# Spatial gating moved from the projection phase into the attention phase of a hybrid encoder step, with attention cut into sections of 1024 keys

## The chip, the cores and the metric

The kernel runs on one core of a Trainium2 chip. The metric is the device time of one launch in microseconds, the median of the runs shown. The program is one straight list of instructions on five queues: PE (TensorE), DVE (VectorE), ACT (ScalarE), POOL (GpSimd) and SP, which issues every DMA. Each queue runs in order. A build-time scheduler puts the instructions of each engine into that order, starting from the order in which the Python code emits them.

## What is computed

One layer on 2176 tokens: 128 sample tokens (8 streams of 16 steps, each with 512 cached keys) and a prompt of 2048 tokens. D_MODEL is 1024, the two head groups are 512 wide each, D_FF is 2816.

```python
h = rms_norm(x); p = h @ w_in                  # columns: u | v | q | k | v of attention, 512 each
u_a = gelu(p[u]); v_a = layer_norm(gelu(p[v]))
out_a = u_a * (tril(W_s) @ v_a + b_s)          # per head of 128, in chunks of 128 tokens
z = q @ k.T / 8                                # 8 heads of 64, strictly causal
log_fail = where(reach, log_sigmoid(-z), 0)
incl = cumsum(log_fail, axis=keys, reverse=True)   # excl: the same, one key later
w = where(reach, exp(log_sigmoid(z) + excl), 0); out_b = w @ v
mix = concat(rms_norm(out_a), rms_norm(out_b)) @ w_out
x = x + rms_norm(mix)
up = causal_conv3(rms_norm(x) @ w_up)
y = x + rms_norm((gelu(up[gate]) * up[val]) @ w_down)
```

The kernel forms the attention weights without logarithms: s = sigmoid(z), S = 1 - s, a running product of S from the last key backwards, and w = s times that product one key later.

## The kernel before

Activations are feature-major (features on the 128 partitions, tokens along the free axis), and the tokens go through in pieces of 384 (the last has 256). A float32 product of the projections is three passes: each operand is split into hi + lo, hi by a cast on ACT and lo by a subtraction on DVE (`weights`, lines 174 and 175, for weight tiles; lines 161 and 162 for the token-major stage).

Phase 1 (from line 287) is a list of jobs; the weights of a job are fetched and split two jobs ahead, and chains of small steps advance one step after each job. For each piece the jobs are: four u jobs (`feature`, evacuated by `evac_u`, lines 396 to 401), eight token-major jobs for the gating values v (`evac_va`, with their LayerNorm), eight for the attention values, then eight feature-major jobs for k and q (`evac_qk`), whose halves are stored to DRAM. `gate_chain` (lines 441 to 470) then does the spatial mixing of the piece on PE (psg, line 447), multiplies by u on DVE, norms the result over its 512 features and stores it, split, to the DRAM array na_s.

Phase 2 (from line 541) is attention. For each of four pairs of heads (hp), query tiles of 128 are taken in the order of `ORDER`, which alternates short and long ones; a unit is one query tile of one head, with up to 2048 keys. A unit has four stages, run as a pipeline over the units: loads four units ahead; `weigh` (line 550); transposes of the weights three units later (line 580); the values of two query tiles and both heads after that (line 715). In `weigh` PE writes scores of 512 keys to PSUM (line 688), ACT takes the sigmoid (line 560), POOL clears the masked triangle of the last 128 keys (`affine_select`, line 692) and writes S = 1 - s (line 563), DVE runs one running product over the whole row (the scan, line 567) and multiplies by s (line 568). The scan reads S twice from SBUF; the multiplication reads s and S; both of POOL's steps read and write SBUF.

Eight sample units, one per stream, stand among the units of the first three head pairs (three, three and two of them). Their values (line 649) multiply weight tiles of 128x128 by 64 columns, in 40 instructions on PE.

Phase 3 is the output projection, its norm and the residual; its first operands come from na_s and from ob_s, the stored attention output (`mix_prep_chain`, line 797). Phase 4 is the convolutional FFN. These two are not changed, but for the name of an array.

Of the kernel before, what the change touches and what calls it, by code (L numbers as in the profile page):

```python
# [21 lines left out]
P = 128  # L22
# [16 lines left out]
ORDER = [0, 8, 9, 1, 10, 2, 11, 3, 12, 4, 13, 5, 14, 6, 15, 7]  # L39
# [13 lines left out]
def hybrid_kernel(ctx: ExitStack, tc: tile.TileContext, a: dict):  # L53
# [27 lines left out]
    # sample queries and keys, split, kept for the sample attention  # L81
    qs = cpool.tile([P, 2, 4, NSAMP], F32R, name="qs")
    ks = cpool.tile([P, 2, 4, NSAMP], F32R, name="ks")

    class Scratch:
        """a DRAM array cut along its token axis, so that a reader waits for its own tokens only."""
# [8 lines left out]
        def parts(self, c0, c1):  # L95
            """(array of those tokens, first, last + 1, counted from c0)"""
# [12 lines left out]
    na_s = dpool.tile([2, 4, P, TOK], F32R, name="na_s")  # L109
# [5 lines left out]
    # Products run as a list of jobs; a job's weights are fetched and split two jobs ahead, and  # L115
    # the chains of small steps (norms, gating) advance by one step after each job.
# [11 lines left out]
    def store(out, in_, then=None, wait=1):  # L128
        """a store, issued some steps later, so that loads behind it don't wait for its data."""
# [27 lines left out]
    def split(pool, src, shape, tag, bufs=None):  # L157
        """src = hi + lo exactly, both in float32r."""
# [19 lines left out]
    def sq_sum(pool, key, acc, src, first, n):  # L178
        """acc[P, n] (+)= sum over the 4 feature tiles of src[P, 4, n] squared."""
# [59 lines left out]
    def sq_step(pool, key, acc, src, first, n, eng=None):  # L239
        """acc[P, n] (+)= src[P, n] squared."""  # L240
# [20 lines left out]
    # keys [hi; lo] of a head and queries, as [hi; hi] and as [lo; lo]; opened when room is there  # L261
# [11 lines left out]
    def key_tile(h):  # L273
        """three tiles take turns; the last heads leave one in kq free early."""
# [3 lines left out]
    def load_queries(h, c):  # L278
        t = kq[0].tile([P, 2, 512], F32R, tag="Q", name="Q", bufs=4)
        for src, o0, o1 in q_s[h // 2].parts(NSAMP + c * 512, NSAMP + (c + 1) * 512):  # L280
# [6 lines left out]
    # ------------------------------------------------------------------ phase 1  # L287
    # input projection, spatial gating; the RMSNorm's row factor is applied to the products
    with ExitStack() as c1:
# [54 lines left out]
        def piece_jobs(pi, H, Hn):  # L344
# [96 lines left out]
            def gate_chain():  # L441
# [18 lines left out]
                for f in range(4):  # L460
# [8 lines left out]
                    if f == 1:  # L469
                        yield  # L470
# [728 lines left out]
```

## Time and profile before

| | us |
|---|---|
| median of three runs (lowest, highest) | 3116.44 (3113.71, 3117.62) |
| span of the profiled execution, first to last instruction | 3110.4 |
| PE busy | 2894.4 (93%) |
| DVE busy | 1962.9 (63%) |
| ACT busy | 1203.9 (39%) |
| POOL busy | 806.8 (26%) |

The profiled execution is known by its span; the median of the runs is 6.0 us more than the span, which is what lies around it. The busy share is an average over phases with different limits: phase 1 ends with the last projection product at 529.6 us, phase 2 with the last attention values at 1259 us, phase 3 near 1500 us. A busy PE is not PE at its peak, since matmuls overlap in the pipeline. Idle time of an engine that is waited for by nobody costs nothing.

### The profile page before, as it was taken

How to read it: one execution, taken by the hardware profiler on the slowest of the kernel's cores; microseconds unless marked ns; L12 is line 12 of the kernel's file. 1: busy time of each engine (PE TensorE's matmuls, PEld its weight loads, DVE VectorE, ACT ScalarE, POOL GpSimd, SP SyncE). 2: the span in 40 equal slices, each digit the busy share in tenths (PEclk: the TensorE clock that was granted, in tenths of full speed). 3: DMA queues.
4: the chain of work that ended last, by engine and by line, in shares of the span. 5: the costliest groups of instructions: out<-in, count | busy, mean ns of one | idle time of the engine just before them, and what ended most of it. 6: DMA issues, size and time to landing. Idle time of an engine off the chain costs nothing.

```text
span 3110.4 us, 43545 instructions
## 1 busy us (share of the span) xinstructions
PE 2894.4 (93%) x17064; PEld 2718.8 (87%) x17064; DVE 1962.9 (63%) x2667; ACT 1203.9 (39%) x2068; POOL 806.8 (26%) x874
## 2 busy tenths in 40 slices
PE   8999997788797786999999999999999999999997
PEld 8999996666676654899999999999999999999997
DVE  6676776878878788586645455673544566344445
ACT  5444443444444354454433223433322243332222
POOL 1000002877858789256100000210000031000002
PEclk9999998788887798999999999999999999999998
DMA  5666677114142310566421221253122224212223
GB/s 203 219 211 223 234 248 213 48 61 109 50 116 62 99 48 21 182 208 222 152 80 53 70 75 62 88 160 100 57 69 72 65 87 130 73 55 68 72 64 105
DMA packets 192542, 352.88 MB, mean 113 GB/s; under 512 B 24785, under 2 KB 116177, under 8 KB 190289
## 3 DMA queue, kind: packets, MB, share of 16 engines
q1 hardware_dynamic: 192336, 350.09, 35.4%
q8 instruction: 135, 2.21, 0.3%
q14 instruction: 71, 0.57, 0.1%
HBM read 286.97 MB, written 63.06 MB: 113 GB/s over the span
## 4 chain that ended last, share of the span: by engine, by line
PE 75%; POOL 10%; DVE 6%; DMA 4%; issue 2%; ACT 1%; SPq 0%; POOLq 0%; ACTq 0%; DVEq 0%
PE pu L258 11%; PE pu L259 11%; PE pu L257 11%; POOL S L563 7%; PE pd L257 5%; PE pd L259 5%; PE pd L258 5%; PE psf L259 3%; PE psf L257 3%; PE psf L258 3%; PE po L649 2%; POOL s L692 2%; PE po L715 2%; PE pst L387 2%; PE pst L389 2%
## 5 line engine op out<-in xcount | busy, mean ns | idle before, releaser
L175 DVE TENSOR_TENSOR wlo<-wr,whi 128x1024 fp32r<-128x1024 f32 (+2 forms) x357 | 392.4, 1100 | 562.3 <-ACT whi L174 560.3
L257 PE MATMUL pu<-hhi,whi 128*128 128x364 f32 (+1 forms) x2112 | 695.6, 329 | 1.0 <-ACT nhs L983 1.0
L258 PE MATMUL pu<-hlo,whi 128*128 128x364 f32 (+1 forms) x2112 | 696.2, 330 | 0.0
L259 PE MATMUL pu<-hhi,wlo 128*128 128x364 f32 (+1 forms) x2112 | 695.8, 330 | 0.4 <-DVE wlo L175 0.4
L174 ACT CAST whi<-wr 128x1024 fp32r<-128x1024 f32 (+2 forms) x357 | 330.5, 926 | 739.0 <-PE pu L258 277.9
L563 POOL TENSOR_SCALAR S<-s 128x512 f32<-128x512 f32 (+4 forms) x336 | 400.3, 1202 | 123.5 <-ACT s L560 100.6
L567 DVE TENSOR_TENSOR_SCAN S<-S 128x256 f32<-128x256 f32 (+16 forms) x136 | 349.6, 2579 | 94.3 <-POOL S L563 67.5
L257 PEld LDWEIGHTS pu<-hhi,whi 128*128 128x128 f32 x2112 | 399.3, 189 | 1.6 <-ACT nhs L983 1.6
L258 PEld LDWEIGHTS pu<-hlo,whi 128*128 128x128 f32 x2112 | 398.6, 189 | 0.2 <-POOL hlo L783 0.2
L259 PEld LDWEIGHTS pu<-hhi,wlo 128*128 128x128 f32 x2112 | 398.0, 188 | 0.8 <-DVE wlo L175 0.7
L257 PE MATMUL pd<-ghi,whi 128*128 128x362 f32 (+3 forms) x1016 | 337.0, 332 | 10.7 <-DVE acc L1019 10.7
L259 PE MATMUL pd<-ghi,wlo 128*128 128x362 f32 (+3 forms) x1016 | 335.9, 331 | 0.0
L258 PE MATMUL pd<-glo,whi 128*128 128x362 f32 (+3 forms) x1016 | 335.8, 331 | 0.0
L586 ACT COPY wT<-pt 128x512 f32<-128x512 f32 (+3 forms) x328 | 165.5, 554 | 339.3 <-PE pt L580 336.0
L971 DVE SCALAR_TENSOR_TENSOR y<-pu,cvec,y 128x726 f32<-128x726 f32 (+2 forms) x352 | 270.0, 777 | 8.7 <-ACT y L968 4.1
L580 PE MATMUL pt<-ident,s 128*128 128x128 f32 (+1 forms) x1128 | 184.7, 308 | 92.3 <-DVE s L568 90.7
L580 PEld LDWEIGHTS pt<-ident,s 128*128 128x128 f32 (+1 forms) x1128 | 147.6, 158 | 123.4 <-issue 95.4
L783 POOL TENSOR_TENSOR hlo<-xp,hhi 128x182 fp32r<-128x182 f32 x32 | 22.2, 699 | 789.0 <-ACT hhi L782 407.9
L257 PEld LDWEIGHTS pd<-ghi,whi 128*128 128x128 f32 x1016 | 193.2, 190 | 14.1 <-DVE acc L1019 7.4
L1019 DVE TENSOR_TENSOR acc<-acc,pd 128x362 f32<-128x362 f32 (+2 forms) x192 | 101.7, 530 | 156.4 <-PE pd L259 155.7
L257 PE MATMUL psf<-hhi,whi 128*128 128x384 f32 (+1 forms) x576 | 191.0, 332 | 10.0 <-ACT hhi L314 7.2
L258 PEld LDWEIGHTS pd<-glo,whi 128*128 128x128 f32 x1016 | 193.2, 190 | 0.3
(173 smaller groups left out, 5083.1 us busy)
## 6 DMA issues: line engine op xcount, KB each, us to landing
wr<-wup SPq DMA_DIRECT2D x132, 512.0 KB, 3.3
wr<-win_f SPq DMA_DIRECT2D x72, 512.0 KB, 4.8
wk<-win_t SPq DMA_DIRECT2D x96, 256.0 KB, 2.8
wr<-wout SPq DMA_DIRECT2D x38, 512.0 KB, 4.1
wr<-wdown SPq DMA_DIRECT2D x72, 256.0 KB, 2.6
x<-xT SPq DMA_DIRECT2D x40, 384.0 KB, 5.6
wr<-wdown SPq DMA_DIRECT2D x48, 320.0 KB, 2.9
Q<-q_s SPq DMA_DIRECT2D x48, 256.0 KB, 8.2
```

Source lines behind the costliest of these rows:

```text
L174: nc.scalar.copy(hi, wr)
L175: nc.vector.tensor_tensor(out=lo, in0=wr, in1=hi.bitcast(F32), op=ALU.subtract)
L257: nc.tensor.matmul(ps, lhsT=whi, rhs=ahi, start=start, stop=False)
L258: nc.tensor.matmul(ps, lhsT=whi, rhs=alo, start=False, stop=False)
L259: nc.tensor.matmul(ps, lhsT=wlo, rhs=ahi, start=False, stop=stop)
L387: nc.tensor.matmul(pss[i], lhsT=hi, rhs=whi, start=(k == 0), stop=False)
L563: nc.gpsimd.tensor_scalar(out=S[:, c0:c0 + cn], in0=s[:, c0:c0 + cn], scalar1=-1.0, scalar2=1.0, op0=ALU.mult, op1=ALU.add)
L567: nc.vector.tensor_tensor_scan(out=R, data0=R, data1=R, initial=1.0, op0=ALU.mult, op1=ALU.bypass)
L580: nc.tensor.transpose(pt[:kn, j], w[:, (j0 + j) * P:(j0 + j) * P + kn], ident)
L586: nc.scalar.copy(wT[:, j0:j0 + full], pt[:, :full])
L971: nc.vector.scalar_tensor_tensor(out=o, in0=i, scalar=w, in1=o, op0=ALU.mult, op1=ALU.add)
L1019: nc.vector.tensor_tensor(out=o, in0=o, in1=src, op=ALU.add)
```

## The change

The u products leave phase 1, and with them `evac_u` and `gate_chain`. Phase 1 now begins each piece with the token-major jobs; the LayerNormed gating values go to a DRAM array va_s, and the row factors of all tokens are kept in the tile rall. In phase 2 a generator `gating` loads the u weights once, splits them with the norm gain folded in, and then takes the 17 token tiles of 128 one by one, token-major: load x, split it, 24 products of 512 columns, a scaling by the row factor, a gelu for three or four tiles at once; `gate_chain` then does mixing, the norm (its mean square by `bn_stats`, its square root on POOL) and a transposition on PE per tile. The generator is advanced between attention units, from the end of the first head pair on, in proportion to the keys that the units hold.

Attention takes the query tiles in pairs (`PAIRS`); a pair with more than 1024 keys is done in two sections of keys, the later keys first; the second section starts its running product from the value that the first left (a copy on DVE, a copy on POOL in place of a memset). All eight sample units stand in the first head pair, one after each pair of query tiles, and use the tiles of the gating generator, which begins after them. Their values go the other way round: weights of 32 columns as the stationary operand, 128 value columns moving, each of four groups into its own 32 partitions; a copy on ACT and one transposition on PE follow.

```diff
+PAIRS = [0, 4, 1, 5, 2, 6, 3, 7]
...
-            for f in range(4):
-                jobs.append(feature(f, lambda ps, f=f: when_ready(lambda: evac_u(f, ps))))
-            jobs += token(1, evac_va)
-            jobs += token(0, evac_v)
+            jobs += token(1, lambda i, ps: when_ready(lambda: evac_va(i, ps)))
+            jobs += token(0, lambda i, ps: when_ready(lambda: evac_v(i, ps)))
...
-        psz = c2.enter_context(tc.tile_pool(name="p2z", bufs=4, space=PSUM, reuse_waits="tile"))
-        pst = c2.enter_context(tc.tile_pool(name="p2t", bufs=3, space=PSUM, reuse_waits="tile"))
+        psz = c2.enter_context(tc.tile_pool(name="p2z", bufs=3, space=PSUM, reuse_waits="tile"))
+        pst = c2.enter_context(tc.tile_pool(name="p2t", bufs=2, space=PSUM, reuse_waits="tile"))
+        psf = c2.enter_context(tc.tile_pool(name="p2g", bufs=2, space=PSUM, reuse_waits="tile"))
...
-            big = W > 1024
-            s = two.tile([P, 2048 if big else 1024], F32, tag="sB" if big else "sS", name="s", bufs=3)
-            S = two.tile([P, 2056 if big else 1032], F32, tag="SB" if big else "SS", name="S")
+            s = two.tile([P, 1024], F32, tag="s", name="s", bufs=4)
+            S = two.tile([P, 1032], F32, tag="S", name="S", bufs=3)
...
-            nc.gpsimd.memset(S[:, W:W + 1], 1.0)
+            if carry is None:
+                nc.gpsimd.memset(S[:, W:W + 1], 1.0)
+            else:
+                nc.gpsimd.tensor_copy(S[:, W:W + 1], carry)
...
+            nc.vector.tensor_tensor_scan(out=R, data0=R, data1=R, initial=1.0 if carry is None else carry,
+                                         op0=ALU.mult, op1=ALU.bypass)
...
+                for j in range(5):
+                    kn = P if j < 4 else NS
+                    for kt in range(4):
+                        cs = slice(kt * P, (kt + 1) * P)
+                        nc.tensor.matmul(po[kt * 32:(kt + 1) * 32], lhsT=wT[:kn, j, kt * 32:(kt + 1) * 32],
+                                         rhs=vc[:, j, cs] if j < 4 else vnew[:, cs], start=(j == 0), stop=(j == 4))
...
+        def gate_chain(i, u):
+            vt = fil.tile([P, 512], F32, tag="va", name="va", bufs=2)
+            load(vt, va_s.parts(i * P, (i + 1) * P)[0][0])
+            yield
+            pm = psf.tile([P, 4, P], F32, tag="pf", name="pm")
+            for h in range(4):
+                nc.tensor.matmul(pm[:, h], lhsT=wst[:, kind, h], rhs=vt[:, h * P:(h + 1) * P], start=True, stop=True)
+            for h in range(4):
+                nc.vector.scalar_tensor_tensor(out=o[:, hs], in0=pm[:, h], scalar=bst[:, kind, h:h + 1],
+                                               in1=u[:, hs], op0=ALU.add, op1=ALU.mult)
+            nc.vector.bn_stats(out=six, in_=o)
+            nc.vector.bn_aggr(out=mv, in_=six)
...
+            nc.gpsimd.tensor_tensor(out=rs, in0=ms, in1=mhalf[:, 0:1], op=ALU.pow)
+            yield
+            nc.vector.scalar_tensor_tensor(out=o, in0=o, scalar=rs, in1=ga, op0=ALU.mult, op1=ALU.mult)
+            yield
+            for h in range(4):
+                nc.tensor.transpose(pt[:, h], o[:, h * P:(h + 1) * P], ident)
+            nc.scalar.copy(nhl[:, 0], pt)
+            nc.vector.tensor_tensor(out=nhl[:, 1], in0=pt, in1=nhl[:, 0].bitcast(F32), op=ALU.subtract)
...
+        def gating():
+            load_gating()
...
+            def fetch(i):
+                load(xr, a["xT"][:, :, i * P:(i + 1) * P])
+                nc.scalar.copy(hi, xr)
+                nc.vector.tensor_tensor(out=lo, in0=xr, in1=hi.bitcast(F32), op=ALU.subtract)
...
+                for k in range(KD):
+                    hi, lo, w = x[0][:, k], x[1][:, k], uw[k]
+                    nc.tensor.matmul(ps, lhsT=hi, rhs=w[:, 0], start=(k == 0), stop=False)
+                    nc.tensor.matmul(ps, lhsT=hi, rhs=w[:, 1], start=False, stop=False)
+                    nc.tensor.matmul(ps, lhsT=lo, rhs=w[:, 0], start=False, stop=(k == KD - 1))
+                    if k % 2:
+                        yield
+                nc.scalar.activation(ub[:, m - n], ps, AF.Copy, scale=rall[:, i:i + 1])
...
+            if begin <= i < len(units):
+                done += units[i][4]
+                while steps * total < NSTEP * done and fill_:
```

The next two pieces are DVE's queue in the attention phase, about the middle of it. Before: scans (L567, S) and multiplications (L568, s) of units alone.

```order
L567 SCALAR_TENSOR_TENSOR S<-S 128x1664
L568 TENSOR_TENSOR s<-s,S 128x512
L568 TENSOR_TENSOR s<-s,S 128x1664
L567 SCALAR_TENSOR_TENSOR S<-S 128x1664
L723 COPY ob<-po 128x256
L568 TENSOR_TENSOR s<-s,S 128x1664
L567 SCALAR_TENSOR_TENSOR S<-S 128x640
L568 TENSOR_TENSOR s<-s,S 128x640
```

Now: L521 and L523 are the scan and the multiplication, L665 the copy of what a section leaves; o, six, mv, ms and nhl belong to one tile's gating, and rs comes from POOL.

```order
L665 COPY left<-S 128x1
L752 BN_AGGR mv<-six 128x2
L754 SCALAR_TENSOR_TENSOR ms<-mv 128x1
L756 TENSOR_SCALAR ms<-ms 128x1
L521 SCALAR_TENSOR_TENSOR S<-S 128x640
L760 SCALAR_TENSOR_TENSOR o<-o,rs,ga 128x512
L523 TENSOR_TENSOR s<-s,S 128x640
L665 COPY left<-S 128x1
L521 SCALAR_TENSOR_TENSOR S<-S 128x768
L699 COPY ob<-po 128x256
```

Scans have become shorter and more, and gating steps stand between them in the same queue; L760 has a step of POOL (rs) to wait for.

The last two pieces are PE's queue around the values of one sample unit; pt are transposes of weights, z scores. Before:

```order
L580 MATMUL pt<-ident,s 128x128 x4
L649 MATMUL po<-wT,vc 128x64 x4
L649 MATMUL po<-wT,vnew 128x64
L649 MATMUL po<-wT,vc 128x64 x4
L649 MATMUL po<-wT,vnew 128x64
L649 MATMUL po<-wT,vc 128x64 x4
L649 MATMUL po<-wT,vnew 128x64
L649 MATMUL po<-wT,vc 128x64 x4
L649 MATMUL po<-wT,vnew 128x64
L580 MATMUL pt<-ident,s 128x128 x9
```

Now:

```order
L603 MATMUL pos<-vc,wTs 32x128 x16
L603 MATMUL pos<-vnew,wTs 32x128 x4
L655 MATMUL z<-K_3545,Q 128x512 x2
L655 MATMUL z<-K_3546,Q 128x512 x2
L608 MATMUL pt<-ident,os 128x128
L674 MATMUL pt<-ident,s 128x128 x10
```

The same 20 products (each two instructions on the engine) now have 32 output rows and 128 moving columns, and one transposition comes after them, behind the scores of other units.

## Rows read from the trace of the kernel before

**Rows 1.** Windows of phases 1 and 2, with their columns.

```profile
core 0: us, PE busy (x) PEld busy (x) DVE busy (x) ACT busy (x) POOL busy (x), PEclk, DMA share, GB/s
7.20:529.60 522.40, 509.98 (x2773) 469.08 (x2774) 362.47 (x666) 240.78 (x379) 30.37 (x33) 0.99 0.68 223
529.60:1245.00 715.40, 554.56 (x3323) 438.02 (x3322) 583.41 (x417) 318.68 (x679) 564.32 (x614) 0.82 0.25 71
```

**Rows 2.** Windows in phase 1: u jobs, token-major jobs, last piece's token-major jobs.

```profile
187.30:203.96 16.66, 16.66 (x99) 16.66 (x97) 9.06 (x14) 7.09 (x12) 0.00 (x0) 1.00 0.85 301
203.96:231.20 27.24, 27.24 (x121) 22.54 (x121) 15.74 (x31) 10.44 (x17) 2.97 (x3) 1.00 0.43 135
...
460.90:498.70 37.80, 30.35 (x114) 20.77 (x113) 17.04 (x31) 11.13 (x18) 1.81 (x2) 0.86 0.80 209
```

**Rows 3.** Groups by line and shape in phase 1, spatial mixing: busy us, mean ns.

```profile
L447 PE MATMUL psg<-wst,va 128*128 128x128 f32 x136 | 18.7, 274 | 0.0
```

**Rows 4.** Windows of the four head pairs, each from its first scan.

```profile
533.00:721.00 188.00, 147.33 (x871) 118.42 (x869) 155.57 (x119) 83.28 (x176) 150.20 (x168) 0.81 0.29 78
721.00:909.00 188.00, 153.18 (x920) 122.10 (x919) 153.03 (x123) 82.73 (x175) 140.76 (x158) 0.82 0.29 79
909.00:1094.00 185.00, 144.19 (x859) 114.59 (x860) 144.80 (x105) 78.56 (x168) 138.26 (x151) 0.81 0.29 81
1094.00:1245.00 151.00, 107.67 (x667) 81.37 (x664) 129.16 (x69) 71.43 (x156) 134.35 (x136) 0.85 0.12 35
```

**Rows 5.** Timeline of five microseconds of attention: start, duration, instruction, idle before.

```profile
1161.35 4.02 DVE L567 TENSOR_TENSOR_SCAN S<-S 128x1664 f32<-128x1664 f32 x1 [0.57 <-POOL S L563]
...
1161.89 3.56 POOL L692 TENSOR_SCALAR_AFFINE_SELECT s<-s 128x128 f32<-128x128 f32 x1
...
1165.88 1.88 DVE L567 TENSOR_TENSOR_SCAN S<-S 128x640 f32<-128x640 f32 x1 [0.51 <-POOL S L563]
```

**Rows 6.** Waits in attention: who, for whom, us, times, longest.

```profile
DVE S L567 <- POOL S L563: 66.1, 57, 5.1
...
DVE S L567 <- POOL S L565: 26.5, 34, 5.3
```

**Rows 7.** Groups by shape in attention: scans of five widths.

```profile
L567 DVE TENSOR_TENSOR_SCAN S<-S 128x2048 f32<-128x2048 f32 x8 | 36.9, 4614 | 21.0 <-POOL S L563 19.0 <-POOL S L565 2.0
...
L567 DVE TENSOR_TENSOR_SCAN S<-S 128x1152 f32<-128x1152 f32 x8 | 20.9, 2614 | 15.1 <-POOL S L563 15.1
...
L567 DVE TENSOR_TENSOR_SCAN S<-S 128x1024 f32<-128x1024 f32 x6 | 14.2, 2371 | 3.2 <-POOL S L565 2.2 <-POOL S L563 1.0
L567 DVE TENSOR_TENSOR_SCAN S<-S 128x640 f32<-128x640 f32 x8 | 13.5, 1688 | 1.1 <-POOL S L563 1.1
...
L567 DVE TENSOR_TENSOR_SCAN S<-S 128x512 f32<-128x512 f32 x8 | 11.8, 1474 | 3.1 <-POOL S L565 3.0
```

**Rows 8.** Groups by shape in phase 1, as prices of the moved steps.

```profile
L175 DVE TENSOR_TENSOR wlo<-wr,whi 128x1024 fp32r<-128x1024 f32 x71 | 86.7, 1222 | 33.4 <-ACT whi L174 33.3
L162 DVE TENSOR_TENSOR wklo<-wk,wkhi 128x512 fp32r<-128x512 f32 x96 | 65.6, 688 | 70.0 <-ACT wkhi L161 70.0
...
L419 POOL TENSOR_TENSOR rs<-ve,mhalf 128x1 f32<-128x1 f32 x17 | 16.1, 948 | 288.8 <-DVE ve L417 288.3
...
L413 DVE BATCH_NORM_STATS2 bst<-va 128x6 f32<-128x512 f32 x17 | 11.2, 684 | 5.1 <-ACT va L406 5.1
...
L221 DVE SCALAR_TENSOR_TENSOR dg<-ident,rstd,dg 128x128 fp32r<-128x128 f32 x34 | 10.1, 347 | 0.0
```

**Rows 9.** Chain that ended last, a sample's values and a prompt's values.

```profile
609.36 10.12 PE po L649 x40
...
624.08 1.69 PE po L715 x16
```

**Rows 10.** Timeline of PE where attention ends and phase 3 begins.

```profile
1255.72 3.76 PE L715 MATMUL po<-wT,V 128*64 128x256 f32 x32
1259.41 0.44 PE L257 MATMUL psm<-ahi,whi 128*128 128x384 f32 x1
```

More of the change, by code (lines that the diff above doesn't have):

```diff
@@ L83, in hybrid_kernel @@
     ks = cpool.tile([P, 2, 4, NSAMP], F32R, name="ks")
+    rall = cpool.tile([P, NTT], F32, name="rall")
     class Scratch:
@@ L108, in hybrid_kernel @@
     v_s = Scratch("v_s", [TOK, 512], 0, LATE)
-    na_s = dpool.tile([2, 4, P, TOK], F32R, name="na_s")
+    va_s = Scratch("va_s", [TOK, 512], 0, LATE)
+    na_s = Scratch("na_s", [2, 4, P, TOK], 3, [p[0] for p in PIECES] + [TOK], F32R)
     ob_s = Scratch("ob_s", [4, P, TOK], 2, [0, NSAMP] + [NSAMP + c * 512 for c in range(1, 5)])
@@ L332, in load_consts @@
             dma(lng, a["ln"])
-            dma(bsp, a["bsp"])
-            nc.gpsimd.memset(wst, 0.0)
-            dma(wst[:, 1], a["wst"])
-            for b in range(NB):
-                dma(wst[b * NS:(b + 1) * NS, 0, :, b * NS:(b + 1) * NS], a["wst"][0:NS, :, 0:NS])
-            for i in range(2):
-                nc.gpsimd.affine_select(out=wst[:, i], in_=wst[:, i], pattern=[[0, 4], [1, P]],
-                                        compare_op=ALU.is_ge, fill=0.0, base=0, channel_multiplier=-1)
             yield
@@ L517, in early @@
                 yield
-                for c in (2, 0):
-                    first["Q", g, c] = load_queries(g, c)
+                for pr in (PAIRS[1], PAIRS[0]):
+                    first["Q", g, pr] = load_queries(g, pr)
                     yield
@@ L527, in early @@
                 yield
-        head = jobs[-24]
-        jobs[-24] = (head[0], lambda w: (chains.append(early()), head[1](w)))
+        head = jobs[-20]
+        jobs[-20] = (head[0], lambda w: (chains.append(early()), head[1](w)))
         ready = [jobs[0][0]()]
@@ L640, in values @@
+                pt = pst.tile([P, 4, P], F32, tag="pt", name="pt")
+                for j in range(4):
+                    nc.tensor.transpose(pt[:, j], w[:, j * P:(j + 1) * P], ident)
+                nc.scalar.copy(wT[:, :4], pt)
+                pt = pst.tile([P, 4, P], F32, tag="pt", name="pt")
+                nc.tensor.transpose(pt[:NS, 0], w[:, PAST:W], ident)
+                nc.scalar.copy(wT[:NS, 4], pt[:NS, 0])
             def values(part):
@@ L702, in transposes @@
-                transposed(st["w"], W, shared["T", t - t % 2, g][:, :, (t % 2) * P:(t % 2 + 1) * P])
+                for j0 in range(b0, b0 + n, 4):
+                    jn = min(4, b0 + n - j0)
+                    if ("T", pr, j0, g) not in shared:
+                        shared["T", pr, j0, g] = two.tile([P, 4, 2 * P], F32, tag="wT", name="wT", bufs=6)
+                    pt = pst.tile([P, 4, P], F32, tag="pt", name="pt")
+                    for j in range(jn):
+                        nc.tensor.transpose(pt[:, j], st["w"][:, (j0 - b0 + j) * P:(j0 - b0 + j + 1) * P], ident)
+                    nc.scalar.copy(shared["T", pr, j0, g][:, :jn, i * P:(i + 1) * P], pt[:, :jn])
@@ L704, in values @@
             def values(part):
-                if g == 0 or t % 2 == 0:
+                if g == 0 or i == 0:
                     return
-                cut = [(t + 1) * i // NPART for i in range(NPART + 1)]
-                if part == 0:
-                    st["po"] = pso.tile([P, 2 * P], F32, tag="po", name="po")
-                po = st["po"]
+                cut = [b0 + n * p // NPART for p in range(NPART + 1)]
+                if part == 0 and own:
+                    shared["po", pr] = pso.tile([P, 2 * P], F32, tag="po", name="po")
@@ L717, in values @@
-                if part < NPART - 1:
+                                         rhs=T[:, (j - b0) % 4, q], start=first_, stop=last)
+                if part < NPART - 1 or b0:
                     return
@@ L741, in hybrid_kernel @@
         stages += [(2, LAG, ())]
+        begin += LAG + 1 + NPART
+        total = sum(u[4] for u in units[begin:-6])
+        fill_, done, steps = gating(), 0, 0
         for i in range(-PRE, len(units) + LAG + 1 + NPART):
@@ L745, in hybrid_kernel @@
                     units[i - lag][stage](*args)
+            if begin <= i < len(units):
+                done += units[i][4]
+                while steps * total < NSTEP * done and fill_:
+                    if next(fill_, StopIteration) is StopIteration:
+                        fill_ = None
+                    steps += 1
+                    tick()
+        while fill_ and next(fill_, StopIteration) is not StopIteration:
+            tick()
+        finish()
     wpools.append(ctx.enter_context(tc.tile_pool(name="w3", bufs=2, reuse_waits="tile", side="right")))
```

290 lines of the change are left out of this document (161 added, 129 removed).

## The prediction, written before the changed kernel ran

> **What bounds the kernel now.** I read the slices of the page first, then windows by phase, then the waits and the timeline inside attention. The windows show two kinds of phase. In phase 1 PE is busy for 510 of 522 us at a granted clock of 0.99: PE is the limit, and a product that leaves it shortens the phase by its own time [rows 1]. In phase 2 no single engine is full: of 715.4 us PE is busy for 554.6, DVE for 583.4, POOL for 564.3, and the clock averages 0.82, a mixture of the levels 1.2 and 2.4 GHz [rows 1]. What ends last there is read from the scans: they waited 66.1 us for POOL's S and 26.5 us for its memset, 92.6 of the 132 us in which DVE was idle [rows 6, 1]. And POOL's busy time is not work. An affine_select began half a microsecond after a scan of 1664 columns and took 3.56 us; it ended as the scan did, and the next scan had waited 0.51 us for POOL [rows 5]. So DVE and POOL take turns: POOL is held while a scan runs, and does its steps in DVE's pauses. Attention is a chain of DVE steps with short POOL steps between, and DVE work added there adds time unless it stands in those pauses.
>
> The four head pairs give the scale. The last, without samples, took 151 us with DVE busy for 129.2; the others took 188, 188 and 185 with three, three and two samples [rows 4]. Taking 151 for each pair, the samples cost 37 + 37 + 34 = 108 us, 13.5 each. The four stretches sum to 712.
>
> **Phase 1, what goes.** The u jobs of a full piece are 96 products, 16.66 us in the window of one piece [rows 2]. Five pieces make 83.3; the last piece has two thirds of the columns, 11.1. The mixing products go too, 18.7 us in all at the most [rows 3]; the DVE and ACT steps beside them were hidden behind PE. That is 113. Against it: the last piece's token-major jobs took 37.8 us, where two tiles at the pace of a full piece (121 products in 27.24 us, and 96 needed) would take 21.6 [rows 2]; they waited for their weights while the early keys and queries were fetched. They will now follow the q and k stores at once, without the u jobs between. I take 5 us more of that wait, between nothing and 11. So **phase 1: -108**.
>
> **Phase 2, what comes.** Per token tile on DVE: the subtraction for xl at the row of 128x1024, 1.222; four mixing steps of 128x128 at 0.347; bn_stats 0.684; three short ones at 0.15, an estimate below the 0.347 row; two steps of 512 columns at 0.688 [rows 8]. Sum 5.12, times 17 is 87. Once: eight weight subtractions at 0.688 and about 14 small steps at 0.347 and a reduction of 1.2, 11 in all. Gating: 98 us of DVE, 32.7 for each of the last three head pairs.
>
> Sections: 64 units become two. A scan of 2048 (4.61) becomes two of 1024 (2.37 each): +0.13. One of 1152 (2.61) becomes 640 and 512 (1.69 + 1.47): +0.55 [rows 7]. The middle, 0.34, times 64 is 22; the multiplications get between nothing and as much again, I take 11; the copies of what is left, 64 at an estimated 0.15, give 10. Some 41 in all, 10 per head pair, with bounds of 4 and 15.
>
> POOL gets 17 square roots at 0.948 [rows 8], 16 us, and copies for memsets. ACT gets some 55 us by like widths, hidden on an engine busy for 319 of 715. PE gets 408 products of 512 columns at 27.24/121 = 0.225 us, 92 us, and 136 small ones as in [rows 3]; PE is idle for 161 us there and not waited for most of the time, so I cost them at nothing; if that cover were gone, up to 110 us would show.
>
> How much of the DVE work hides: of the 5.12 us per tile, the mixing, bn_stats, the short steps and the last subtraction, 3.2 us, read at most one operand from SBUF (the other comes from PSUM), 18 us per head pair. In the queue they stand between scans, where DVE was waiting for POOL (23 us per head pair, by rows 6). Bounds: nothing, and all 21.8 us of idle time of a pair without samples. I take four fifths of 18, 14.5. The subtraction for xl and the norm's product read two SBUF operands like the scans, and add in full. Head pairs two to four: 151 + 10 + 32.7 - 14.5 = 179 each.
>
> Samples: the value block of one took 10.12 us on PE, 40 instructions [rows 9]. Attention's own values, in column halves, issue 16 instructions of 256 columns in 1.69 us, 0.106 each [rows 9]. Forty at that pace are 4.2 us, 5.9 less; the bounds are 0.25 of that (four groups at once, half the columns) and the old 10.1. A copy, a transposition and tiles without a second buffer cost about 1.9 (estimate; between nothing and 5). So 9.5 each, and the first head pair takes 151 + 10 + 76 = 237. The sum is 237 + 3 x 179 = 774 against 712. **Phase 2: +62**, with bounds of 690 (no added time, samples at 4) and 864 (nothing hidden, samples dearer): -22 and +152.
>
> The Trainium skill, in TensorEngine Tiling (Array Packing), Key Properties, says that tiles run independently and in parallel, but that changing the tiling mode drains the engine. The row of column halves agrees with the first; no run here shows four groups. By full parallelism the block would be near 1 us and the forecast about 24 us lower; by a drain at each change a little higher.
>
> **Where attention ends.** Before, the first product of phase 3 came 3.7 us after the last group of values began, with no gap, since its operands had been fetched and normed ahead [rows 10]. Now those operands go where the gating tiles lie, and the last tile's norm and transposition come with the last units; a load, four squares, a norm and four splits then lie open. All of it in the open would be some 16 us (an estimate, by steps of half a microsecond and one landing); half can go beside the last values, so I take 8, between nothing and 16.
>
> **Sum.** -108 + 62 + 8 = -38 on the profiled execution's span of 3110.4; the median lies 6.0 above that span, and 3116.4 - 38 gives 3078. I say 3079.
>
> **Rivals.**
> (B) Phase 2 keeps its length. All the added DVE work falls into idle time, of which there are 132 us [rows 1], and the time is 3017: DVE's 583 + 98 + 41 less some small copies is 714, and with 10 us of ramps phase 2 is 724, +9, with nothing lost at its end: -99. For it: steps that take an operand from PSUM may leave POOL free, and the samples' stalls end. Against it: 92.6 of the 132 us are waits for POOL, whose work has to go somewhere, and the steps with two SBUF operands hold it up. Beside it stands a rule of the Trainium skill, SBUF — State Buffer, Who interferes with whom: a DVE instruction with two SBUF inputs contends with a GpSimd instruction that reads SBUF, for its whole length, and one with at most one such input, outside the two-port modes, does not. By the first half the scans hold POOL, and the trace agrees (3.56 us); the second half, no row here shows by itself.
>
> (C) Slower. Each tile's chain goes twice through queues that are full: rs through POOL, then the transposition on PE, with DVE's next step waiting in order, and the scans behind it. If nothing of the DVE work hides (+43.5) and each of 17 tiles makes DVE wait for a held POOL step of 3.56 us (+60) [rows 5], the time is 3183. It decides from 38 us on, which is 2.2 us per tile. For it: in-order queues and a POOL held by scans. Against it: in the new order a scan or a multiplication often stands between the step before rs and the one that takes it.
>
> (D) The four groups don't overlap, and the samples' fetches, now into single buffers, stall the pair instead: samples cost 15 each, 44 more, and the time is 3123.
>
> (E) Phase 1 doesn't give what was removed, since its transfers bind. The u window moved 301 GB/s at a share of 0.85, 5.0 MB, of which the u weights (2.1) and na_s (1.6) go; 1.3 MB and 0.8 of va_s fall on the token-major window, which moved 3.7 MB at 135 GB/s: it would come to 213, under what the u window bore [rows 2]. Against it too. At a saving of 60 the time is 3127.
>
> **How the numbers follow.** Forecast 0.48, B 0.20, C 0.18, D 0.08, E 0.06. About 0.2% (6 us) is what a measurement of this kernel can tell from no change. Faster: 0.43 of the forecast's 0.48, B's 0.20 and 0.03 of D and E, 0.66. Same: 0.03 of the forecast, 0.02 of C, 0.05 of D and E, 0.10. Slower: the rest, 0.24. The forecast's own range is 3045 to 3112. The whole range goes from 3005, below B, to 3150, which leaves out the upper half of C and a little below B.
>
> **What would show it.** Phase 1's last projection product should come near 422 us, from 529.6; by E it comes after 460. The stretch from there to the first product of phase 3 should be near 800 us; by B under 745, by C over 850. DVE should be busy for about 705 of it, with waits of the scans for POOL below 92 us in spite of more scans; by C waits of L760 for rs and of L767 for PE stand high in the list. The value block of a sample should take 2 to 5 us; by D it takes ten. The head pair with all samples should take about 237 us and the others about 179. PE's granted clock in phase 2 should rise over 0.82; that by itself is worth little here. The forecast is wrong if phase 2 grows by less than 20 us or by more than 105, or if phases 3 and 4, which I take as unchanged, move by more than 10 us after the first projection product.

## The result, and the profile after

The changed kernel took 3059.9 us (median; 3055.9 to 3061.3) against 3115.5 (3113.7 to 3117.6): ratio 0.982, interval 0.981 to 0.984, 55.6 us less. The profiled execution's span went from 3110.4 to 3054.1. Forecast were 3079 and -38 for the span; the sign and the two large terms came out, but two costs inside the second were wrong, in opposite directions.

First the two phases by windows, the answer to [rows 1]: from the first product to the last projection product, and from there to the first product of phase 3. The columns are start and end, length, busy time (and instructions) of PE, PE's weight loads, DVE, ACT and POOL, then granted clock, DMA share, GB/s.

```profile
6.00:416.30 410.30, 394.02 (x2016) 353.66 (x2016) 263.11 (x477) 186.83 (x284) 23.13 (x27) 0.98 0.74 238
416.30:1199.60 783.30, 659.12 (x4061) 465.77 (x4060) 686.65 (x792) 394.94 (x780) 528.31 (x708) 0.93 0.36 99
```

Phase 1 ends 113.3 us earlier (529.6 to 416.3) and is still PE's. The stretch after it grew from 729.8 (529.6 to 1259.4, [rows 10]) to 783.3: +53.5. What follows takes 1854.5 us in place of 1851.0, so the sum is -113.3 + 53.5 + 3.5 = -56.3. In the stretch PE is now busy for 84% and DVE for 88%, at a clock of 0.93 after 0.82; no run separates what the higher clock is worth.

The four head pairs, to be read against [rows 4] (the fourth ends at attention's last product):

```profile
425.80:633.70 207.90, 166.05 (x1200) 121.38 (x1201) 184.05 (x213) 99.99 (x208) 147.12 (x200) 0.89 0.42 122
633.70:810.40 176.70, 152.53 (x899) 105.05 (x896) 151.06 (x140) 92.77 (x185) 132.08 (x161) 0.95 0.31 81
810.40:998.00 187.60, 170.79 (x979) 121.19 (x978) 170.93 (x209) 97.02 (x188) 124.47 (x169) 0.96 0.36 98
998.00:1190.00 192.00, 167.81 (x982) 117.00 (x980) 171.25 (x217) 97.37 (x189) 119.79 (x166) 0.95 0.28 81
```

Forecast were 237 and three times 179. The pair with all samples is 29 us shorter than that. The later ones took 176.7, 187.6 and 181.5, 9 more together: the 181.5 go to the end of the last scan, where [rows 4] stop too.

DVE's waits from the first scan to attention's end, the answer to [rows 6] (who, for whom, us, times, longest):

```profile
DVE S L521 <- POOL S L514: 43.5, 63, 3.1
DVE o L760 <- POOL rs L758: 7.2, 12, 1.2
DVE S L521 <- POOL S L517: 7.0, 10, 2.1
```

The scans wait 50.5 us for POOL in place of 92.6, in spite of 64 more of them; the norm's wait for rs, the core of the prediction's rival C, is 7.2.

A sample's values on PE, against the 10.12 us of [rows 9], then the end of attention, against [rows 10] (start, duration, instruction, idle before):

```profile
471.47 1.08 PE L603 MATMUL pos<-vc,wTs 128*32 128x128 f32 x32 [1.27 <-DVE ob L699]
472.48 0.42 PE L603 MATMUL pos<-vnew,wTs 16*32 16x128 f32 x8
...
1183.82 5.03 PE L691 MATMUL po<-wT,V 128*64 128x256 f32 x30
1188.78 0.66 PE L764 MATMUL pn<-ident,o 128*128 128x128 f32 x4
1199.59 0.66 PE L260 MATMUL psm<-ahi,whi 128*128 128x384 f32 x1 [10.14 <-DMA ahi<-na_s]
```

The 40 products take 1.43 us. Behind the last tile's transposition PE stands for 10.1 us for phase 3's first operands, where before there was no gap.

### The profile page after: what moved, and what is told of

The parts are those of the page before. It is cut to its first block, busy times and chain, and to the rows that moved or that the text cites. A ratio compares the mean times of both kernels' runs of the same rounds, so it can differ in the third digit from the quotient of the medians.

```text
span 3054.1 us, 43907 instructions
## 1 busy us (share of the span) xinstructions
PE 2868.9 (94%) x16934; PEld 2622.4 (86%) x16934; DVE 1959.1 (64%) x2845; ACT 1219.9 (40%) x2063; POOL 762.5 (25%) x957
## 4 chain that ended last, share of the span: by engine, by line
PE 75%; DVE 8%; POOL 6%; DMA 4%; issue 4%; ACT 2%; SPq 1%; POOLq 0%; DVEq 0%; ACTq 0%
PE pu L261 11%; PE pu L260 11%; PE pu L262 11%; PE pd L260 5%; PE pd L261 5%; PE pd L262 5%; POOL S L514 4%; DVE S L521 3%; PE po L691 2%; PE pt L674 2%; PE psf L262 2%; PE psf L260 2%; PE psf L261 2%; PE pst L379 2%; PE psm L260 2%
## 5 line engine op out<-in xcount | busy, mean ns | idle before, releaser
L178 DVE TENSOR_TENSOR wlo<-wr,whi 128x1024 fp32r<-128x1024 f32 (+2 forms) x333 | 362.8, 1090 | 577.5 <-ACT whi L177 575.4
L177 ACT CAST whi<-wr 128x1024 fp32r<-128x1024 f32 (+2 forms) x333 | 305.2, 917 | 732.1 <-PE pu L261 277.4
L514 POOL TENSOR_SCALAR S<-s 128x512 f32<-128x512 f32 (+4 forms) x336 | 324.2, 972 | 147.0 <-ACT s L511 115.5
L521 DVE TENSOR_TENSOR_SCAN S<-S 128x896 f32<-128x896 f32 (+8 forms) x136 | 237.1, 1745 | 39.9 <-POOL S L514 32.8
L675 ACT COPY wT<-pt 128x512 f32<-128x512 f32 (+3 forms) x320 | 161.7, 528 | 202.8 <-PE pt L674 202.1
L674 PEld LDWEIGHTS pt<-ident,s 128*128 128x128 f32 x1088 | 135.6, 151 | 119.4 <-issue 59.7
L674 PE MATMUL pt<-ident,s 128*128 128x128 f32 x1088 | 182.4, 298 | 58.6 <-DVE s L523 16.8
L523 DVE TENSOR_TENSOR s<-s,S 128x640 f32<-128x640 f32 (+7 forms) x200 | 197.4, 991 | 8.2
L655 PE MATMUL z<-K,Q 128*128 128x512 f32 (+3 forms) x640 | 191.6, 407 | 7.4 <-ACT s L511 5.0
```

The source lines that it names most:

```text
L177: nc.scalar.copy(hi, wr)
L178: nc.vector.tensor_tensor(out=lo, in0=wr, in1=hi.bitcast(F32), op=ALU.subtract)
L514: nc.gpsimd.tensor_scalar(out=S[:, c0:c0 + cn], in0=s[:, c0:c0 + cn], scalar1=-1.0, scalar2=1.0, op0=ALU.mult, op1=ALU.add)
L521: nc.vector.tensor_tensor_scan(out=R, data0=R, data1=R, initial=1.0 if carry is None else carry, op0=ALU.mult, op1=ALU.bypass)
L523: nc.vector.tensor_tensor(out=s[:, :W], in0=s[:, :W], in1=S[:, 1:W + 1], op=ALU.mult)
L655: nc.tensor.matmul(z, lhsT=Q[:, j, i * P:(i + 1) * P], rhs=K2[:, b0 * P + c0:b0 * P + c0 + cn], start=(j == 0), stop=(j == 1))
```

## The experiments

Four theories on what sets gating's price in attention are told apart, by letters of their own (not those of the prediction's rivals). A is the forecast's: DVE work that is not hidden. B: nothing, it falls into idle time. C: the products in PE's in-order queue. D: ACT, waiting in order for loads. Differences below are between medians; the kernel before moved between 3111.6 and 3115.5 from job to job.

**Gating left out.** `gating()` only stores zeros to na_s.

> Leaves the gating out of attention altogether (na_s is filled with zeros); sections and sample values stay as changed. Theory A (my prediction): gating adds 98 us of DVE work to attention of which a good half stays visible (about 55 us), and some 8 to 10 us at the boundary come from its last tile: about 2995 us, and a stretch from the last projection product to the first product of phase 3 of about 720 us, close to the 730 of the kernel before. Theory B: gating's work falls into idle time, and what made the stretch longer than before is the sections; then the stretch stays at 765 or more and the time at 3040 or above.

Measured: 2974.0 us, 0.955 of before (0.953 to 0.957). The whole stretch, and head pairs one to four (the fourth up to the first product of phase 3), then the end on PE:

```profile
415.90:1120.70 704.80, 560.72 (x3440) 378.62 (x3439) 609.61 (x579) 333.02 (x701) 557.97 (x687) 0.88 0.32 90
420.10:631.60 211.50, 169.42 (x1208) 123.70 (x1210) 182.74 (x203) 101.86 (x212) 153.29 (x203) 0.88 0.41 120
631.60:791.60 160.00, 126.24 (x751) 82.30 (x751) 140.78 (x124) 73.72 (x160) 138.51 (x161) 0.91 0.46 132
791.60:952.00 160.40, 128.44 (x722) 83.88 (x721) 140.61 (x121) 75.01 (x160) 133.01 (x161) 0.88 0.21 56
952.00:1120.70 168.70, 135.25 (x757) 87.92 (x756) 142.91 (x123) 79.64 (x165) 130.42 (x156) 0.86 0.15 44
```

```profile
1116.61 4.20 PE L691 MATMUL po<-wT,V 128*64 128x256 f32 x30
1120.75 0.45 PE L260 MATMUL psm<-ahi,whi 128*128 128x384 f32 x1
```

B falls: gating costs 86 us of time, and A's 2995 was 21 too high. Sections and samples alone make the stretch 25 us shorter than before. A pair without samples takes 160 (forecast 151 + 10), and a sample (211.5 - 160) / 8 = 6.4 (forecast 9.5). Gating then costs the later pairs 16.7, 27.2 and 32.9 us, the last with the boundary's 10; here there is no gap.

**Only the u products** (weights, inputs, products, GELU; mixing and norm out, na_s zero).

> Keeps gating's u products (weights, input split, 408 products of 512 columns, GELU) between attention units and leaves out the mixing, norm and transposition of every tile (na_s is filled with zeros). Theory A (DVE sets the price): the u products bring 21 us of DVE splits of 17 plus 7 us of weight splits, the left-out chain about 4 us of DVE per tile, 68 us; so of the gap between this change and the kernel without gating most belongs to the chain: about 3015 us, 20 above the kernel without gating. Theory C (PE sets the price): PE was busy for 659 of the 774 us of attention, the u products are 100 us or more of that and the chain only 20, so nearly the whole gap stays: about 3045 us.

Measured: 3049.0 (0.979; 0.978 to 0.981), where C stood: 75 above the kernel without gating. But this is no clean subtraction. Where gating begins, twenty scans take 93.0 us here and 65.0 without gating; the complete kernel takes 76.6 for them. The whole stretch and those scans, then four lines of SP's queue there (start and duration), then some waits of the whole stretch:

```profile
414.60:1187.80 773.20, 649.03 (x3848) 450.61 (x3847) 627.49 (x604) 384.98 (x757) 525.60 (x687) 0.91 0.35 96
668.00:761.00 93.00, 72.33 (x371) 49.16 (x365) 66.06 (x63) 40.73 (x81) 52.98 (x69) 0.87 0.36 100
```

```profile
643.17 8.18 SPq L136 DMA_DIRECT2D na_s<-nhl  x10
...
652.32 16.51 SPq L136 DMA_DIRECT2D na_s<-nhl  x18
...
672.72 4.70 SPq L136 DMA_DIRECT2D na_s<-nhl  x6
...
709.05 0.37 SPq L64 DMA_DIRECT2D ur<-win_f  x1
```

```profile
POOL S L514 <- ACT s L511: 150.0, 63, 19.3
...
ACT xh L728 <- DMA xr<-xT: 41.7, 13, 8.1
```

The zeros of na_s wait for no result, and all their 34 stores stand between the loads of the u weights. The last of these loads is issued at 709.1 us, in the complete kernel at 696.2. Every kernel with u products and zeros is long there, so some 17 of the 75 us (93.0 less 76.6) very likely belong to the zeros, though no run separates it. Without them this kernel would stand between A and C.

The waits suggested D: ACT stands for an input load, and the sigmoids behind it are late. Three kernels test it.

**A third of the u products; no split of the input; one input for all tiles**, each made from the kernel with the u products alone:

```
-matmul(ps, hi, w[:, 0]); matmul(ps, hi, w[:, 1]); matmul(ps, lo, w[:, 0])
+matmul(ps, lo, w[:, 0])                     # a third
-nc.vector.tensor_tensor(out=lo, in0=xr, in1=hi, op=ALU.subtract); return hi, lo
+return hi, hi                               # no split
-nxt = fetch(i + 1) if i + 1 < NTT else None
+nxt = x                                     # one input
```

> The kernel with the u products only (no mixing and norm), and of its three products of each 128x128 weight block one is kept, that of the split-off low part: 272 of 408 products of 512 columns are left out, every input split on DVE and ACT, every load and every GELU stay. The u products brought 75 us (2974 to 3049). Theory C (their PE time stands in PE's in-order queue ahead of the units' products): two thirds of it goes, about 3000 us. Theory A (the input splits on DVE and the waits for them set the price): it stays at 3040 to 3050.

> The kernel with the u products only, without the subtraction that makes the low part of the input (17 times 1.26 us on DVE, two operands in SBUF); the third product takes the high part again, so that PE's work is the same. Theory C (PE's queue sets the price): within 8 us of 3049. Theory A (DVE sets it): 21 us of DVE go and with them 15 to 21 us, about 3030.

> The kernel with the u products only, in which all 17 tiles multiply the first tile's input: 16 input loads, casts on ACT and subtractions on DVE are left out, and all 408 products and the GELUs stay. With every part it took 3049, without gating 2974, without the subtraction 3042, with a third of the products 3028. Theory D (ACT waiting for the loads is the largest part): about 3005 to 3015. Theory C (PE's products are): 3035 to 3042.

Measured: 3027.7 (0.973; 0.971 to 0.974), 3042.4 (0.977; 0.976 to 0.979) and 3051.3 (0.980; 0.979 to 0.982). The first stands between the ranges of A and C, the second within C's, the third above both of its own. The stretches of a third and of one input:

```profile
415.70:1172.00 756.30, 595.42 (x3576) 405.15 (x3575) 630.76 (x604) 383.14 (x758) 544.22 (x687) 0.89 0.35 98
```

```profile
414.60:1192.50 777.90, 640.40 (x3848) 449.12 (x3846) 607.01 (x588) 369.85 (x742) 514.00 (x687) 0.91 0.30 85
```

Two thirds of the products less give 21.3 for 54 us of PE, less than half of what C said (3000). The subtraction alone gives 6.6. Sixteen loads, casts and subtractions less (20 us of DVE, 15 of ACT) seem to gain nothing. But with nothing to wait for, the products of this kernel stand in another order: in one block, not spread over three head pairs. The first of each three products (durations in ns, first and last start in us) with the u products alone and with one input, then the window of that block:

```profile
L742 PE MATMUL pu<-uw,xh x136: 387/393/775, 722.2 to 1101.7; 128*128 128x512 f32 x136
```

```profile
L742 PE MATMUL pu<-uw,xh x136: 388/392/735, 723.4 to 895.6; 128*128 128x512 f32 x136
723.40:896.40 173.00, 173.00 (x927) 130.71 (x928) 94.62 (x85) 81.68 (x144) 59.71 (x114) 1.00 0.16 39
```

In the block PE is busy for all of 173.0 us: there its queue is the limit, as C says. What the loads cost where the products are spread, this kernel doesn't show.

**Loads ahead**, in the complete kernel: a second buffer for the loaded input (and for the u weights and cached keys, which use the same tile), the cast and split three steps after the load.

> The changed kernel, complete, with the inputs of the u products loaded ahead: the tile they land in gets a second buffer, the load is issued at a tile's start, and the cast on ACT and the subtraction on DVE come three steps later. In the changed kernel ACT stood 50.7 us before the casts for these loads and 12.3 for those of the u weights, with the sigmoids and copies of the attention units queued behind. Theory D (ACT's in-order queue hands that wait on to the units): most of it goes, 25 to 45 us off, 3015 to 3035. Theory C (PE's queue alone sets what gating costs): within 8 us of 3060.

Measured: 3062.9 (0.984; 0.982 to 0.986), no gain. ACT's waits for the inputs fell only from 50.7 to 42.5 us, so the wait was moved rather than taken away. No kernel here takes it away and leaves the rest in its place: D is neither shown nor refuted.

**Only the chain:** mixing, norm, transposition and split of all 17 tiles, on a tile of ones, without the u products.

> The changed kernel without gating's u products, their weights, inputs and GELUs: mixing, norm, transposition and split of all 17 tiles stay in their places between the units and take a tile of ones for u. DVE keeps 72 us of the chain, PE 32 us of mixing products and transpositions. Without any gating it is 2974, with all of it 3060; without the chain it was 3049, but that kernel also stalled some 20 us longer where gating begins. Theory A (my forecast: DVE work adds what is not hidden, about 45 to 55 us with the boundary's 8): 3015 to 3030. Theory C (PE's queue sets the price and DVE's chain hides): 2980 to 2995, of which 8 at the boundary. If the parts simply add, 2985; if they replace one another, well above it.

Measured: 3012.1 (0.968; 0.967 to 0.970), 38 above no gating and between A and C. Head pairs two, three, and four up to attention's last product, then the end on PE:

```profile
632.40:794.10 161.70, 128.52 (x775) 84.37 (x774) 140.96 (x128) 75.11 (x162) 140.85 (x161) 0.91 0.22 56
794.10:959.20 165.10, 131.83 (x793) 91.01 (x792) 159.09 (x189) 77.13 (x166) 131.81 (x168) 0.91 0.31 83
959.20:1136.60 177.40, 140.31 (x865) 99.12 (x863) 163.70 (x204) 81.84 (x172) 135.25 (x164) 0.89 0.26 76
```

```profile
1134.68 1.94 PE L691 MATMUL po<-wT,V 128*64 128x256 f32 x14
...
1148.12 1.08 PE L764 MATMUL pn<-ident,o 128*128 128x128 f32 x4 [4.17 <-DVE o L760]
```

In the third pair DVE has 18.5 us more to do than without gating (159.1 against 140.6) and the pair takes 4.7 longer: 13.8 are hidden. Most of this kernel's 38 is its end: phase 3 begins at 1158.7, 22 us behind the last values, since the last tiles' chains and then the loads stand in the open. In the complete kernel only 10 of such an end are left. Beside it, the complete kernel's third pair is 22.5 us longer (187.6), with 39 us more of PE and 12 of DVE.

The two parts alone cost 75 and 38, 27 more than the 86 of both. The head pairs show where the 27 lie (us, by the starts of their first scans; the fourth to the end of its last scan):

| | second | third | fourth |
|---|---|---|---|
| no gating | 160.0 | 160.4 | 158.4 |
| u products only | 193.5 | 179.5 | 173.6 |
| chain only | 161.7 | 165.1 | 166.6 |
| complete | 176.7 | 187.6 | 181.5 |
| u products only, a third of them | 190.6 | 174.2 | 164.0 |
| u products only, one input | 203.6 | 189.9 | 158.8 |

In the third and fourth pairs, where both parts run, their costs add: 19.1 + 4.7 against 27.2, and 15.2 + 8.2 against 23.1. The surplus is, in the main, the second pair with the u products alone (17 us more than the complete kernel) and the 12 us by which the chain's end is longer alone. So the parts don't hide behind one another here. In these two pairs the u products cost 34.3 us, and 19.4 with a third of them.

**Sample values in the old form**, full weight tiles and 64 moving columns, with the small copies that go with it.

> Only the sample values go back to full 128-column weight tiles with 64 moving columns (40 instructions in a block, 8 small DVE copies for a sample). In the changed kernel a block takes 1.43 us, before it took 10.12. Theory A: nothing else can run in PE's queue meanwhile, and the units behind wait, so that most of 8 x 8.7 us, less the copy and transposition that the new form adds, comes back: plus 35 to 60 us, 3095 to 3120. Rival: PE is not what ends last in attention, and the blocks hide beside DVE's scans: plus 0 to 12 us, 3060 to 3072.

Measured: 3084.4 (0.990; 0.988 to 0.992): plus 24.5, between the two. The first pair grew from 207.9 to 228.7, 2.6 us a sample, and its clock fell from 0.89 to 0.83. The block itself grew from 1.43 us to between 5.6 and 10.1, by the clock that it met; some of it hides. Windows around the fastest and the slowest block (the last three columns are the granted clock, the DMA share and GB/s):

```profile
498.20:503.80 5.60, 5.60 (x43) 5.06 (x41) 4.32 (x3) 2.38 (x4) 5.27 (x4) 1.00 1.02 358
554.90:565.00 10.10, 10.10 (x41) 9.16 (x42) 7.77 (x7) 1.02 (x1) 3.64 (x4) 0.50 0.41 132
```

At 2.4 GHz (1.00) it takes 5.6 us, at 1.2 (0.50) 10.1. The 10.12 of [rows 9] were also taken at 0.50.

**Sections of 512.**

```
-left = 4 if n <= 12 else 8; return [(left, n), (0, left)]
+return [(b, min(b + 4, n)) for b in range(0, n, 4)][::-1]
```

> Sections of 512 keys at most, in place of 1024: 80 sections a head pair in place of 48, 128 more in all, and 128 more carries. Theory A (my prediction's price of 0.64 us for one more section, on DVE's path): plus 80 us, 3140. Rival: shorter scans give POOL back sooner, so that the price is mostly regained: within 25 us of the changed kernel, 3040 to 3085.

Measured: 3094.2 (0.993; 0.992 to 0.995): plus 34.3 for 128 sections, 0.27 us each. The forecast's 0.64 was too high, the rival's 25 too low.

**The carry on ACT:** `nc.scalar.copy(S[:, W:W + 1], carry)`.

> The 64 copies of a section's carry into the next section's tile go from POOL to ACT. On POOL one took 1.02 us, 65.5 us in all, where the memset that it replaced took 0.10. Theory: scans wait 50.5 us for POOL in the changed kernel, and a shorter queue there takes 10 to 25 us off: about 3045 us. Rival: what ends last in attention is PE's queue and the chain through it, and POOL's copies lie in pauses: within 5 us of 3060.

Measured: 3058.4 (0.982; 0.980 to 0.984), as the rival said. The copies' group in the changed kernel and here:

```profile
L519 POOL COPY S<-left 128x1 f32<-128x1 f32 x64 | 65.5, 1024 | 17.4 <-DVE left L665 15.7 <-DVE s L523 1.4
```

```profile
L519 ACT COPY S<-left 128x1 f32<-128x1 f32 x64 | 12.7, 199 | 55.4 <-DVE left L665 48.2 <-DVE s L523 4.1 <-POOL s L659 3.1
```

The copies' 65 us leave POOL, and its busy time in the stretch falls by 39 (528 to 490): its other steps grew, affine_select from 876 to 971 ns. The scans still wait as long for POOL's S (44.8 us, after 43.5). The copies lay in pauses.

**Two pools for gating**, so that phase 3's first operands can be loaded over the u weights before attention ends; the samples' cached keys move with the u weights.

> The gating's weights and inputs, whose last product is 75 us before attention ends, get a pool of their own, which lies under phase 3's first operands; the tiles of mixing and norm lie in a second one. The loads of phase 3's first operands then stand ahead of the last stores in the queue. Theory: the gap of 10 us on PE between attention's last product and phase 3's first goes nearly whole: 3050 to 3054 us, first product of phase 3 within 2 us of the last of attention. Rival: the norm of the attention half, which needs the same loads and is not ready, takes the gap's place: 3057 to 3060.

Measured: 3066.5 (0.985; 0.983 to 0.986), slower than without it, outside both ranges. The gap did go; the values now run into phase 3:

```profile
1199.65 1.94 PE L692 MATMUL po<-wT,V 128*64 128x256 f32 x14
1201.52 0.44 PE L260 MATMUL psm<-ahi,whi 128*128 128x384 f32 x1
```

```profile
PE rb L229 <- DVE dg L221: 9.8, 5, 6.6
```

But phase 3's products now last 226.8 us, not 216.7: they wait for a norm (the second fence, waits in phase 3; in the changed kernel that one is 1.9). The gap's 10 us moved a few products on. And attention's last values came 11 us later; 9 of these lie in the first head pair (217.2 us after 207.9), and no run here explains them.

**S from ACT**, on top of the loads ahead: S = sigmoid(-z) from PSUM, POOL keeping the last 128 columns of a section.

```
+nc.scalar.activation(S[:, c0:c0 + m], z[:, :m], AF.Sigmoid, scale=-1.0)
```

> As the kernel with loads ahead, and besides S = 1 - s comes for all but the last 128 columns of a section from ACT, as the sigmoid of -z straight from PSUM, in place of POOL from s. POOL loses some 240 us of busy time, ACT gains some 150, and is then busy for about 540 of 770 us. Theory: the scans' 50 us of waits for POOL go and the chain of a unit is a step shorter: 20 to 50 us below the kernel with loads ahead. Rival: ACT, in order and with wT copies, casts and sigmoids in one queue, becomes what ends last: the same or up to 40 us slower than that kernel.

Measured: 3017.5 (0.970; 0.968 to 0.971), 45 below the kernel with loads ahead and 42 below the changed one: it beats both kernels. The stretch, and the scans' waits for POOL in it:

```profile
413.80:1158.90 745.10, 654.39 (x4067) 452.86 (x4065) 635.34 (x790) 509.14 (x1083) 279.69 (x508) 0.96 0.38 106
```

```profile
DVE S L526 <- POOL S L522: 28.4, 28, 4.8
DVE S L526 <- POOL S L519: 21.4, 24, 2.8
```

The gain came, but not as the theory said: the scans still wait 49.8 us for POOL, now for the memset and the last 128 columns. What fell is DVE's own time: it does the same work in 635 us in place of 687. Groups by shape on DVE, the changed kernel and this one (count, then busy us and mean ns):

```profile
L521 DVE TENSOR_TENSOR_SCAN S<-S,left 128x1024 f32<-128x1024 f32 x32 | 79.5, 2483 | 11.2 <-POOL S L514 10.7 <-POOL S L517 0.4
...
L523 DVE TENSOR_TENSOR s<-s,S 128x1024 f32<-128x1024 f32 x56 | 74.8, 1338 | 1.8
...
L747 DVE SCALAR_TENSOR_TENSOR o<-pm,bst,ub 128x128 f32<-128x128 f32 x68 | 19.0, 336 | 0.0
...
L760 DVE SCALAR_TENSOR_TENSOR o<-o,rs,ga 128x512 f32<-128x512 f32 x17 | 15.9, 938 | 7.2 <-POOL rs L758 7.2
...
L750 DVE BATCH_NORM_STATS2 six<-o 128x6 f32<-128x512 f32 x17 | 11.4, 670 | 0.0
```

```profile
L526 DVE TENSOR_TENSOR_SCAN S<-S,left 128x1024 f32<-128x1024 f32 x32 | 75.1, 2346 | 6.0 <-ACT S L517 5.9
...
L528 DVE TENSOR_TENSOR s<-s,S 128x1024 f32<-128x1024 f32 x56 | 68.7, 1226 | 3.8 <-POOL s L664 0.4
...
L752 DVE SCALAR_TENSOR_TENSOR o<-pm,bst,ub 128x128 f32<-128x128 f32 x68 | 19.0, 340 | 0.7 <-PE pm L748 0.7
...
L765 DVE SCALAR_TENSOR_TENSOR o<-o,rs,ga 128x512 f32<-128x512 f32 x17 | 12.9, 758 | 6.2 <-POOL rs L763 5.2 <-POOL S L522 0.8
...
L755 DVE BATCH_NORM_STATS2 six<-o 128x6 f32<-128x512 f32 x17 | 11.5, 676 | 0.1
```

With less POOL work beside it the norm's product, two operands in SBUF, falls from 938 to 758 ns and the long multiplication from 1338 to 1226; the mixing step, which takes pm from PSUM, and bn_stats, with one operand, stay. With loads ahead alone the four take 969, 1322, 337 and 672 ns, so the loads are not the cause. This bears out both halves of the rule weighed in the prediction (the Trainium skill, SBUF — State Buffer, Who interferes with whom).

## Why the prediction was right or wrong, by its steps

- **Phase 1, -108: right.** Measured -113.3. The 5 us that I added for the last piece's token-major jobs did not come: they took 33.4 us (350.4 to 383.8), 4.4 less than before, 2.1 of that the mixing products that had stood among them.
- **Transfers in phase 1 (rival E): refuted.** The last projection product came at 416.3, far from 460.
- **Samples, 9.5 us each: mis-sized.** 6.4 by the kernel without gating, 25 us less in the first pair. The block takes 1.43 us, not 4.2: the bound by full overlap, which I set aside for the row of column halves, was the nearer one. And the 10.12 us of the old block, from which the working starts, were a price at the low clock; at 1.00 it is 5.6. The old form costs 24.5 us of time, 3.1 a sample; a sample became 7.1 cheaper (13.5 to 6.4), and where the other 4 come from no run separates. Rival D erred the other way.
- **Sections, +10 per pair: the sum held, its working less so.** (Its terms, 22, 11 and 10, give 43 and not 41; nothing hangs on it.) A pair takes 160, and 158.4 to the end of its last scan, where the 151 stop. But a section costs 0.27 us by the sections of 512, 4.3 for the 16 of a pair. What makes the other 3 isn't separated.
- **Gating's DVE work, 18.2 us visible per pair: near in sum by luck, wrong in cause.** Measured 16.7, 27.2 and 23.1, 12 more in all. The chain hides far better than I said: I took 14.5 of 32.7, and of 18.5 us in the third pair 13.8 were hidden. So rival B was nearer on DVE's chain. That the pairs still grew is the u part's doing, whose products I had left out of the sum.
- **The u products on PE, "I cost them at nothing": this step failed.** I named the cover, PE's idle time, and what was at stake if it was gone. Idle time of an in-order queue is no cover by itself: z, transpositions and values of the next units stand behind the products. In the complete kernel the u part costs 3059.9 - 3012.1 = 48 us. Of the u part alone, two thirds of the products carry 21 and the input's split 7. That the products cost by standing in PE's queue is shown where they stand in one block and PE is full; for the spread ones it is argued. What carries the rest, ACT's waits for the loads among it (D), isn't settled. The stall of some 17 us where the u products begin belongs to the kernel with zeros and not to the change.
- **Boundary, +8: right**, 10.1. That it can simply be filled was not so: its time came back in phase 3.
- **Rival C: refuted.** Waits for rs are 7.2 us; the scans' waits for POOL fell.
- **POOL's carry copies, which I gave no price: 65.5 us of its time**, and nothing in the total.

The span's -56 against -38 is thus 5 from phase 1 and 25 from the samples on one side, and gating's 12, the boundary's 2 and 3.5 behind attention on the other; the 6 us left over lie in sections and ramps. So the forecast came near partly by luck: two misses of opposite sign in phase 2.

## What to carry to other kernels

Price work put into the gaps of a chain on each in-order queue that it enters, not by the engine's idle share: ask what stands behind it there. Before a difference between kernels with parts left out is read as a price, look window by window where it lies: here the zeros that took a part's place made a stall of their own, and leaving out the loads put the products in another order. Where neither was the case, the parts' costs added. And when DVE and POOL share long stretches, look for POOL steps that ACT can do from PSUM: here that was worth 42 us, more than any other change tried on the complete kernel.

## What the runs showed of the hardware that was not expected

- Four groups of 32 weight columns: 40 products of 128 columns in 1.43 us, 0.036 each, against 0.106 for two groups with 256 columns [rows 9] and 5.6 us for the same block with full tiles, all at a granted clock of 1.00. The idle time ahead of the block is put down to DVE's copy of ob; a drain at the change of tiling does not stand out by itself.
- A copy of 128x1 took 1.02 us on POOL and 0.20 on ACT; the memset in its place before took 0.10.
- POOL and DVE slow each other both ways: POOL's affine_select of 128x128 fell from 1155 ns before to 876 with sections of 1024 and 517 with sections of 512, and to 657 with S on ACT. In that last kernel DVE's steps with two tiles from SBUF fell by 3% (xl, 1258 to 1218) to 19% (the norm's product), the scan of 1024, which reads one tile twice, by 6%.
